# Four diagonal taps instead of six for the last two convolution tiles, output weight casts behind the operands' high halves, and four more low halves made in layer 0

## The chip, the cores and the metric

The kernel runs on one core of a Trainium2 chip. The metric is device time in microseconds for one execution on that core; three runs of the kernel before are shown, and one more execution was profiled.

## The reference, cut to what matters

One sequence of 512 tokens and width 1024 goes through two layers, all in float32. Layer 0 has a state-space branch and an attention branch behind one input projection (`e_w_in`) and one output projection (`e_w_out`, from 2048 to 1024 columns). Layer 1, in which most of the change lies, is this:

```python
def conformer_conv_layer(x, g_pre, w_in, conv_w, conv_b, ln_g, ln_b, w_out, g_post):
    u = rmsnorm(x, g_pre)
    proj = jnp.einsum('bsd,de->bse', u, w_in)                 # 1024 -> 3 x 2048
    val, glu_gate, z = jnp.split(proj, [D_CONV, 2 * D_CONV], axis=-1)
    h = val * jax.nn.sigmoid(glu_gate)
    h = causal_depthwise_conv(h, conv_w, conv_b)              # 31 taps in each of 2048 channels
    h = jax.nn.silu(layernorm(h, ln_g, ln_b))                 # over the 2048 channels of a token
    h = h * jax.nn.silu(z)
    out = jnp.einsum('bse,ed->bsd', h, w_out)                 # 2048 -> 1024
    return x + rmsnorm(out, g_post)
```

## The kernel before, in words

**Split products.** A float32 product is made of three matmuls in a faster 32-bit format (`mm3`): each operand is split into a high half, which is a cast on ACT, and a low half, which is the operand less that cast, a subtraction on DVE or POOL. The matmuls are high times high, high times low, low times high. For weights the cast is `w<-wr` (or `ws<-wr` in smaller tiles), from the raw tile `wr` that a DMA brings, and the subtraction is `w<-wr,w` (line 189). For the operands of the output projections the halves are `hlh` and `hll` (function `hilo`, line 119).

**Jobs.** The weights come in tiles of 128 x 1024 (512 KB). Each is a `Job`, and `run` takes the jobs in order, feeding PE in chunks; `split_to` makes the halves of the next jobs and `load_to` issues their loads on SP's queue. Three raw tiles are held at a time, so a raw load waits until the job three places earlier has been cast and subtracted. There are seven large weight tiles; two of them hold gates of layer 1 for a while. A weight tile can also have its low half made ahead: `lo_ahead`, a generator of which `run` takes a step every so many chunks in layer 0, loads a raw tile (`pre`, three buffers), casts it (`prh`), subtracts in place (`pre<-pre,prh`) and stores the result in DRAM (`lo`). In layer 1 such a job loads its low half from there (`w<-lo`) and needs only the cast. This is done for the 48 jobs of `o_w_in`. What is left over of the generator runs at the end of layer 0. A `pre` load waits until the store three places earlier has left its buffer.

**Order.** PE keeps the order in which the program is written. The other engines' rows are placed by a scheduler that goes by priority and dependence; `tc.issue_after(x)` keeps an instruction behind `x`. `cast` puts a weight cast behind the PSUM evacuation (`evacuated`) of three jobs before.

**Layer 1's convolution.** Channels lie in 16 tiles of 128. The 31 taps of a tile are divided: DVE runs `acc<-h,cw,acc` (line 982) on a PSUM accumulator, two tiles interleaved; POOL adds products that ACT makes (`acc<-acc,prod`, line 889), `NPT` counts these; and for the last two tiles, 14 and 15, PE runs `NPE` = 6 taps as matmuls with a diagonal matrix `dg` that ACT makes (`tap_job`; `acc<-h,dg` in float32). Such a tile's PE result is copied by ACT and added by POOL (line 897). The parts are joined in `cvo` (line 987), squared on ACT (line 996), and summed into `Ssum` and `Qsum` (line 1005).

**Statistics and output projection.** PE's `st` matmuls add up the sums over the channels. DVE and POOL make mean and reciprocal deviation from them, PE spreads these over the partitions (`mu`, `rs`), and between these steps PE runs the last three of the `z` jobs. Then each tile goes through `lnorm` (two DVE instructions, lines 1080 and 1081, and a silu on ACT, `s<-cvo`), `lgate` (POOL, `s<-s,sz`, line 1086) and `hilo`. The 16 output jobs, called job 0 to job 15 here, take two of these operands each in the first eight. The first four use small weight tiles (`ws`).

**Layer boundary.** At the end of layer 0 the output projection's last five jobs run together, 128 tokens (a block) after the other. Each block is then normed: its square sum on ACT, `y` (line 708), the variance `var` (line 344), a power on POOL, the residual (line 712, spilled to DRAM), another norm that gives `u` (line 365). PE transposes `u` (`uT`), ACT and DVE take the halves `uh` and `ul` (lines 390, 397), and layer 1 starts. Blocks 0 and 1 are transposed before the last matmuls of block 3.

Of the kernel before, what the change touches and what calls it, by code (L numbers as in the profile page):

```python
# [36 lines left out]
def trunk(  # L37
# [7 lines left out]
    V, G, A, T = nc.vector, nc.gpsimd, nc.scalar, nc.tensor  # L45
    x, out = x[0], out[0]
    e_w_in, e_w_out, o_w_in, o_w_out = e_w_in[0], e_w_out[0], o_w_in[0], o_w_out[0]
# [14 lines left out]
    LA = 6  # L62
    LB = 5
    LC = 3
# [4 lines left out]
    def nm(s):  # L69
        uid[0] += 1  # L70
        return f"{s}_{uid[0]}"

    def t2(s, dt=F32):
        return tp.tile([P, S], dt, tag="t", name=nm(s))
# [4 lines left out]
    def bank(s):  # L79
        return pp.tile([P, S], F32, tag="b", name=nm(s))  # L80
# [4 lines left out]
    def f32(t):  # L85
        return t.bitcast(F32)
# [27 lines left out]
    def tok(b):  # L114
        return slice(b * P, (b + 1) * P)

    def split(hi, lo, src, hi_eng, lo_eng):
        hi_eng(hi, src)
        lo_eng.tensor_tensor(lo, src, f32(hi), ALU.subtract)  # L119

    def hilo(src, n=S, eng=None, s="hl", cast=None):
        h, l = t2(s + "h", F32R)[:, :n], t2(s + "l", F32R)[:, :n]
        split(h, l, src, cast or A.copy, eng or V)
        return h, l
# [13 lines left out]
    def unspill(d, s):  # L138
        t = t2(s)
        nc.sync.dma_start(t, d)  # L140
        return t
# [1 line left out]

    last_load, last_cast = [None], [None]

    evacs = []

    def evacuated(i):
        evacs.append((state["run"], i.ins))

    def cast(hi, src):
        done = [i for n, i in evacs if n <= state["split"] - 3]
        if done:
            with tc.issue_after(done[-1]):
                last_cast[0] = A.copy(hi, src).ins  # L155
        else:
            last_cast[0] = A.copy(hi, src).ins  # L157
# [19 lines left out]
    def wsplit(j):  # L177
        _, _, nk, _, n = j.spec
        hl = j.hl if j.lo is not None else wtiles(j.small)
        w = 1024 // len(hl[0])  # L180
        for i in range(len(hl[0])):
            src = j.raw[:, i * w : (i + 1) * w]
            if j.lo is not None:
                cast(hl[0][i], src)
            else:
                cast(hl[0][i], src)
                for c in range(0, w, S if j.eng is G else w):
                    sl = slice(c, c + (S if j.eng is G else w))
                    j.eng.tensor_tensor(hl[1][i][:, sl], src[:, sl], f32(hl[0][i])[:, sl], ALU.subtract)  # L189
        m = w // n  # L190
        return [lambda k, t=t: t[k // m][:, k % m * n : (k % m + 1) * n] for t in hl]

    def lo_ahead(js):


        def load(j):
            w, r0, nk, c0, n = j.spec
            t = ep.tile([P, 1024], F32, tag="e", name=nm("pre"))
            with tc.issue_after(last_load[0]):
                nc.sync.dma_start(t.rearrange("p (k f) -> p k f", k=nk),  # L200
                                  w[r0 : r0 + nk * P, c0 : c0 + n].rearrange("(k p) f -> p k f", p=P))
            return t

        def sub(t):
            h = eh.tile([P, 1024], F32R, tag="eh", name=nm("prh"))
            for i in range(2):
                sl = slice(i * S, i * S + S)
                with tc.issue_after(last_cast[0]):
                    A.copy(h[:, sl], t[:, sl])  # L209
                V.tensor_tensor(t.bitcast(F32R)[:, sl], t[:, sl], f32(h)[:, sl], ALU.subtract)  # L210

        def store(j, t):
            j.lo = lop.tile([P, 1024], F32, tag="lo", name=nm("lo"))
            nc.sync.dma_start(j.lo, t)
        loaded = []
        for i in range(len(js) + 2):
            if i > 1:
                sub(loaded[i - 2])
            if i > 2:
                store(js[i - 3], loaded[i - 3])  # L220
            if i < len(js):
                loaded.append(load(js[i]))
            yield
        store(js[-1], loaded[-1])

    jobs = []
    state = dict(loaded=0, split=0, run=0)
    ahead = {}

    class Job:  # L230
        def __init__(self, w, r0, nk, c0, n, run, eng=None):
            self.spec, self.run, self.make = (w, r0, nk, c0, n), run, None if w is not None else eng
            self.lo = None
            jobs.append(self)
            self.eng = eng or (V if len(jobs) % 2 else G)
            self.small = False
            if w is not None and eng is V and len(jobs) % 16 in GLO:
                self.eng = G
# [21 lines left out]
    def chunks():  # L260

        i = state["run"]
        split_to(i + 1)
        first = True
        for _ in jobs[i].run(*jobs[i].w):
            if first:
                split_to(i + 1 + ahead.get(i, 2))
                first = False
            yield
        state["run"] = i + 1  # L270

    early = iter(())
    done = {}
# [54 lines left out]
    def run(n, after=None):  # L328

        for _ in range(n):  # L330
            for c, _ in enumerate(chunks()):
                if after is not None:
                    after()
                i = state["run"]
                if 5 <= i < 13 or 26 <= i:
                    if (8 * i + c) % (16 if i >= JO else 7 if i >= 26 else 8) == 0:
                        next(early, None)


# [420 lines left out]
    JO = len(jobs)  # L760
    out_proj(e_w_out, [(lambda k: hilo(yT.pop(k) if k < KT else oT.pop(k - KT), eng=G if k < KT else V), 2)],
             16, gpost, resid0, done0, {(3, 7): start1, (2, "end"): 1, (3, "end"): 1})
    J1 = len(jobs)
# [4 lines left out]
    acc, hs, part, pv, sz = {}, {}, {}, {}, {}  # L768
    sums = []
    NPS = [0] * 8  # L770
    NPT = [10]*7+[8]
    NPE = [0]*7+[6]
    PACE_DVE = 1.03
    PACE_POOL = 0.45
    LEAD = 8
# [67 lines left out]
    def tap_job(j):  # L843

        n = NPE[j // 2]

# [19 lines left out]
    def pool_adds(js, s0, n, init):  # L866

        a2 = {}
        prs = {}

        def prod(i):
            if i < n * len(js):
                j, s = js[i % len(js)], s0 + i // len(js)
                prs[i] = t2("prod")
                A.activation(prs[i][:, s:], hs[j][:, : S - s], AF.Copy, scale=w31(30 - s, j))  # L875
        for j in js:
            a2[j] = t2("acc2")
            if init:
                A.activation(a2[j], hs[j], AF.Identity, bias=c1[:, o_cb1 + j : o_cb1 + j + 1], scale=w31(30, j))
            else:  # L880
                s = s0 + n
                A.activation(a2[j][:, :s], ones[:, :s], AF.Identity, scale=0.0)
                A.activation(a2[j][:, s:], hs[j][:, : S - s], AF.Copy, scale=w31(30 - s, j))
        for i in range(3):
            prod(i)
        for i in range(n * len(js)):
            prod(i + 3)
            j, s = js[i % len(js)], s0 + i // len(js)
            G.tensor_tensor(a2[j][:, s:], a2[j][:, s:], prs.pop(i)[:, s:], ALU.add)  # L889
            yield  # L890
        for j in js:
            if NPE[j // 2]:
                while ("t", j) not in pacc or clock[0] < pacc["t", j] + 1:
                    yield
                pr = t2("prod")
                A.copy(pr[:, 1:], pacc[j][:, 1:])
                G.tensor_tensor(a2[j][:, 1:], a2[j][:, 1:], pr[:, 1:], ALU.add)
                yield
            part.setdefault(j, []).append((a2[j], clock[0]))

    def pool_halves(js):

        n = NPT[0] - 1
        s1 = n + 1
# [28 lines left out]
    def pool_stream():  # L933
        yield from pool_halves((0, 1))
        for j in range(2, NT):
            while j not in hs or clock[0] < hs["t", j] + (3 if j > 1 else 0):
                yield
            yield from pool_adds((j,), 1 + NPE[j // 2], NPT[j // 2] - 1, False)

# [5 lines left out]
    def lane(l):  # L945
        for j in range(l, NT, 2):
            if j < 2:
                m = NPT[0]
                a, b = bank("acc"), c1[:, o_cb1 + j : o_cb1 + j + 1]
# [19 lines left out]
            h = hs[j]  # L969
            n, m, e = NPS[j // 2], NPT[j // 2], NPE[j // 2]  # L970
            s = n + m + e + 1
# [19 lines left out]
    def tile_end(j, a):  # L991
        o = acc[j]
        if not NPT[j // 2]:
            A.copy(o, a)
# [39 lines left out]
    for j in range(NT):  # L1034
        val_job(j)
        gate_job(j)
        while zi < min(NT, j - LEAD + 2):
            z_job(zi)
            zi += 1
    rest = [j for j in range(NT) if NPE[j // 2]]  # L1040
    while zi < NT or rest:
# [5 lines left out]
    JO1 = len(jobs)  # L1047
# [28 lines left out]
    act1 = {}  # L1076
# [8 lines left out]
    def lgate(j):  # L1085
        G.tensor_tensor(act1[j], act1[j], sz[j], ALU.mult)

    def done1(b, y1):
        for f in range(2):
            nc.sync.dma_start(out[tok(b), f * S : (f + 1) * S], y1[f])  # L1090

    out_proj(o_w_out, [(lnorm, LA), (lgate, LB), (lambda j: hilo(act1.pop(j)), LC)],
             NT, gpost1, lambda b: [unspill(d, "x1") for d in x1[b]], done1, {})


# [410 lines left out]

    for j in jobs[6:40]:
        j.eng = G
    early = lo_ahead([j for j in jobs[J1:] if not j.make][:48])
    run(1)  # L1510
    steps = Steps()
    steps.until = JO + 3
# [82 lines left out]
```

## Time and profile before

| | us |
|---|---|
| three runs | 942.18, 944.03, 947.37 (median 944.03) |
| the profiled execution | 945.71 |
| its span | 943.9 |
| PE busy | 909.5 (96%) |
| PE weight loads busy | 754.9 (80%) |
| DVE busy | 730.7 (77%) |
| ACT busy | 601.2 (64%) |
| POOL busy | 506.5 (54%) |
| DMA | 159.84 MB, mean 169 GB/s |

The profiled execution's own time is 1.8 us above its span, since the span runs from the first to the last instruction. A row of the timeline gives start, duration, engine, line, instruction, tile written and tiles read, the shape, and how many alike were put together; in square brackets stands how long the engine was idle ahead of it and what ended that. Matmuls overlap each other, so the durations of single matmuls add up to more than the time that passes, and their start times are what to read. Layer 0 runs to about 563 us, the convolution to about 816, the output projection from 843 on.

### The profile page before, as it was taken

Reading aid. Unit: us, or ns where it says so; the run is one execution under the profiler, and the core shown is the slowest. Engines: PE = TensorE matmul, PEld = TensorE weight load, DVE = VectorE, ACT = ScalarE, POOL = GpSimd, SP = SyncE. Lnnn points to the kernel's source line nnn. Section 1 sums busy time; section 2 is a strip of 40 time slices with the busy share of each in tenths; the row PEclk is TensorE's granted clock in tenths of the full one; section 3 lists DMA queues with packets and bytes.
Section 4 is the critical chain, followed back from the end, with each engine's and each line's share of the span. In section 5 each row is a group of like instructions: output and inputs, shape, how many; then the busy total and the mean of one; then the engine's idle time right before and its main releaser. Section 6 shows DMA issues by size and latency. Waiting matters only on the chain.

```text
span 943.9 us, 13899 instructions
## 1 busy us (share of the span) xinstructions
PE 909.5 (96%) x4691; PEld 754.9 (80%) x4691; DVE 730.7 (77%) x1278; ACT 601.2 (64%) x1128; POOL 506.5 (54%) x474
## 2 busy tenths in 40 slices
PE   6999999998999999999899999999999999998997
PEld 5987787787898888788678889888888887785785
DVE  5657968778977887988776257999999999589602
ACT  5757667567846766576675437787876869456400
POOL 2604554535642444345573114898999999346410
PEclk9999999999999999999999999999999999999999
DMA  6726632347764574664347993565565664425303
GB/s 208 230 73 186 194 90 66 91 144 236 222 214 146 179 241 141 201 225 163 130 144 248 322 320 104 169 191 160 184 211 160 212 194 127 157 76 170 134 1 111
DMA packets 180267, 159.84 MB, mean 169 GB/s; under 512 B 7708, under 2 KB 151716, under 8 KB 180196
## 3 DMA queue, kind: packets, MB, share of 16 engines
q1 hardware_dynamic: 180180, 158.96, 53.0%
q8 instruction: 37, 0.61, 0.3%
q14 instruction: 34, 0.28, 0.1%
q10 hardware_dynamic: 16, 0.00, 0.0%
HBM read 129.45 MB, written 29.36 MB: 168 GB/s over the span
## 4 chain that ended last, share of the span: by engine, by line
PE 45%; DVE 7%; issue 3%; ACT 1%; DMA 1%; POOL 1%; DVEq 0%; POOLq 0%; ACTq 0%
PE m L102 28%; PE o L102 14%; DVE hll L119 1%; PE acc L102 1%; DVE w L189 1%; DVE pre L210 1%; PE tm L102 1%; DVE cvo L1081 1%; PE s L102 1%; DVE cvo L1080 1%; DMA pre<-in_o_w_in_dram 0%; PE pT L106 0%; ACT pr L95 0%; DMA wr<-in_e_w_out_dram 0%; DMA lo<-pre 0%
## 5 line engine op out<-in xcount | busy, mean ns | idle before, releaser
L102 PE MATMUL m<-uh,w 128*128 128x512 f32 (+1 forms) x1392 | 452.6, 392 | 0.4 <-DVE w L189 0.4
L102 PEld LDWEIGHTS m<-uh,w 128*128 128x128 f32 x1392 | 260.8, 189 | 51.4 <-issue 3.1
L102 PE MATMUL m<-ul,w 128*128 128x512 f32 (+1 forms) x696 | 267.3, 384 | 0.0
L189 POOL TENSOR_TENSOR w<-wr,w 128x512 fp32r<-128x512 f32 x112 | 158.7, 1441 | 159.0 <-ACT w L157 123.3
L982 DVE SCALAR_TENSOR_TENSOR acc<-h,cw,acc 128x490 f32<-128x490 f32 (+14 forms) x272 | 177.9, 738 | 3.4 <-ACT acc L974 2.6
L889 POOL TENSOR_TENSOR acc<-acc,prod 128x505 f32<-128x505 f32 (+12 forms) x122 | 156.3, 1283 | 8.1 <-ACT prod L875 0.8
L102 PEld LDWEIGHTS m<-ul,w 128*128 128x128 f32 x696 | 131.9, 189 | 21.3 <-issue 0.5
L102 PE MATMUL o<-w,hlh 128*128 128x512 f32 x448 | 141.4, 397 | 2.7 <-ACT pr L95 2.3
L210 DVE TENSOR_TENSOR pre<-pre,prh 128x512 fp32r<-128x512 f32 x96 | 83.0, 879 | 34.7 <-ACT prh L209 34.4
L102 PEld LDWEIGHTS o<-w,hlh 128*128 128x128 f32 x448 | 82.8, 189 | 19.2 <-ACT pr L95 3.1
L102 PE MATMUL tm<-w,uh 128*128 128x256 f32 (+1 forms) x384 | 91.7, 330 | 1.9 <-ACT pr L95 0.9
L157 ACT CAST w<-wr 128x1024 fp32r<-128x1024 f32 x72 | 74.8, 1048 | 28.6 <-PE o L102 7.9
L1457 POOL TENSOR_SCALAR pr<-pr,ri 128x128 f32<-128x128 f32 (+1 forms) x64 | 40.0, 626 | 92.8 <-DVE ri L1456 87.2
L102 PE MATMUL o<-w,hll 128*128 128x512 f32 x224 | 88.0, 393 | 0.8 <-DVE hll L119 0.8
L209 ACT CAST prh<-pre 128x512 fp32r<-128x512 f32 x96 | 56.8, 622 | 34.6 <-DVE pre L210 12.4
L875 ACT ACTIVATE prod<-h,cw 128x505 f32<-128x505 f32 (+12 forms) x122 | 77.7, 708 | 0.0
L346 POOL TENSOR_TENSOR rstd<-var,mhalf 128x1 f32<-128x1 f32 (+1 forms) x20 | 13.6, 680 | 112.4 <-DVE var L344 112.4
L155 ACT CAST w<-wr 128x1024 fp32r<-128x1024 f32 x56 | 57.4, 1051 | 18.9 <-PE o L102 11.8
L102 PEld LDWEIGHTS tm<-w,uh 128*128 128x128 f32 x384 | 62.8, 190 | 7.6 <-ACT pr L95 1.1
L102 PE MATMUL tm<-w,ul 128*128 128x256 f32 (+1 forms) x192 | 61.2, 319 | 0.0
L95 ACT ACTIVATE pr<-s,nmx 128x128 f32<-128x128 f32 (+1 forms) x64 | 33.9, 530 | 37.4 <-DVE nmx L1451 28.2
L102 PEld LDWEIGHTS o<-w,hll 128*128 128x128 f32 x224 | 42.3, 189 | 11.0 <-DVE hll L119 2.0
(270 smaller groups left out, 1607.1 us busy)
## 6 DMA issues: line engine op xcount, KB each, us to landing
wr<-in_e_w_in_dram SPq DMA_DIRECT2D x56, 512.0 KB
pre<-in_o_w_in_dram SPq DMA_DIRECT2D x48, 512.0 KB
lo<-pre SPq DMA_DIRECT2D x48, 512.0 KB
wr<-in_o_w_in_dram SPq DMA_DIRECT2D x48, 512.0 KB
w<-lo SPq DMA_DIRECT2D x44, 512.0 KB
wr<-in_e_w_out_dram SPq DMA_DIRECT2D x16, 512.0 KB
wr<-in_o_w_out_dram SPq DMA_DIRECT2D x16, 512.0 KB
x<-in_x_dram SPq DMA_DIRECT2D x12, 256.0 KB
```

What stands on the lines that cost most here:

```text
L95: i = A.activation(*a, **kw)
L102: T.matmul(o, l, r, start=start, stop=stop, skip_group_check=True)
L155: last_cast[0] = A.copy(hi, src).ins
L157: last_cast[0] = A.copy(hi, src).ins
L189: j.eng.tensor_tensor(hl[1][i][:, sl], src[:, sl], f32(hl[0][i])[:, sl], ALU.subtract)
L209: A.copy(h[:, sl], t[:, sl])
L210: V.tensor_tensor(t.bitcast(F32R)[:, sl], t[:, sl], f32(h)[:, sl], ALU.subtract)
L346: mark["rstd"] = G.tensor_tensor(r, v, mhalf.to_broadcast([P, ss.shape[-1]]), ALU.pow).ins
L875: A.activation(prs[i][:, s:], hs[j][:, : S - s], AF.Copy, scale=w31(30 - s, j))
L889: G.tensor_tensor(a2[j][:, s:], a2[j][:, s:], prs.pop(i)[:, s:], ALU.add)
L982: V.scalar_tensor_tensor(a[:, s:], h[:, : S - s], w31(30 - s, j), a[:, s:], ALU.mult, ALU.add)
L1457: G.tensor_scalar(p[:, :L], p[:, :L], ri, 1.0, ALU.mult, ALU.mult)
```

## The change

Three edits, and a fourth that paces the third. `NPE` goes from 6 to 4 for the last two tiles and `NPT` from 8 to 9. So DVE's first tap of these tiles is one earlier, and POOL has one more product. The casts of the output weights are placed behind the high half that was issued last (`act_last`), in place of an evacuation three jobs before. And `lo_ahead` is given four more tiles, the output jobs 4 to 7, with a step every 11 chunks in place of 16 in the output projection of layer 0.

```diff
-    evacs = []
+    evacs, act_last = [], [None]
...
     def cast(hi, src):
         done = [i for n, i in evacs if n <= state["split"] - 3]
+        if state["split"] >= JO1 and act_last[0] is not None:
+            done = act_last
         if done:
             with tc.issue_after(done[-1]):
                 last_cast[0] = A.copy(hi, src).ins
...
-                    if (8 * i + c) % (16 if i >= JO else 7 if i >= 26 else 8) == 0:
+                    if (8 * i + c) % (11 if i >= JO else 7 if i >= 26 else 8) == 0:
                         next(early, None)
...
-    NPT = [10]*7+[8]
-    NPE = [0]*7+[6]
+    NPT = [10] * 7 + [9]
+    NPE = [0] * 7 + [4]
...
+    def lparts(j):
+        def high(h, src):
+            act_last[0] = A.copy(h, src).ins
+        return hilo(act1.pop(j), cast=high)
+
...
-    out_proj(o_w_out, [(lnorm, LA), (lgate, LB), (lambda j: hilo(act1.pop(j)), LC)],
+    out_proj(o_w_out, [(lnorm, LA), (lgate, LB), (lparts, LC)],
              NT, gpost1, lambda b: [unspill(d, "x1") for d in x1[b]], done1, {})
...
-    early = lo_ahead([j for j in jobs[J1:] if not j.make][:48])
+    early = lo_ahead([j for j in jobs[J1:JO1] + jobs[JO1 + 4 : JO1 + 8] if not j.make])
```

Lines of the changed kernel are two to seven higher than those named above. Three places show how rows move.

DVE in the output projection, from low half 3 on. Before (`w_9203`, `w_9334`, `w_9381` and `w_9424` are the weights of jobs 4 to 7):

```order
L189 TENSOR_TENSOR w_9203<-wr_9130,w_9203 128x1024
L119 TENSOR_TENSOR hll_9216<-s_9083,hlh_9215 128x512
L1081 TENSOR_TENSOR cvo_8469<-cvo_8469,rs_9062 128x512
L189 TENSOR_TENSOR w_9334<-wr_9167,w_9334 128x1024
L119 TENSOR_TENSOR hll_9237<-s_9092,hlh_9236 128x512
L189 TENSOR_TENSOR w_9381<-wr_9206,w_9381 128x1024
L119 TENSOR_TENSOR hll_9258<-s_9101,hlh_9257 128x512
L1080 TENSOR_TENSOR cvo_8640<-cvo_8640,mu_9057 128x512
L189 TENSOR_TENSOR w_9424<-wr_9337,w_9424 128x1024
L119 TENSOR_TENSOR hll_9279<-s_9201,hlh_9278 128x512
```

The same place in the changed kernel, again from low half 3 on:

```order
L119 TENSOR_TENSOR hll_9254<-s_9117,hlh_9253 128x512
L1083 TENSOR_TENSOR cvo_8505<-cvo_8505,rs_9096 128x512
L1083 TENSOR_TENSOR cvo_8676<-cvo_8676,rs_9096 128x512
L119 TENSOR_TENSOR hll_9275<-s_9126,hlh_9274 128x512
L1082 TENSOR_TENSOR cvo_8773<-cvo_8773,mu_9091 128x512
L1082 TENSOR_TENSOR cvo_8916<-cvo_8916,mu_9091 128x512
L119 TENSOR_TENSOR hll_9296<-s_9135,hlh_9295 128x512
L1083 TENSOR_TENSOR cvo_8773<-cvo_8773,rs_9096 128x512
L1083 TENSOR_TENSOR cvo_8916<-cvo_8916,rs_9096 128x512
L119 TENSOR_TENSOR hll_9317<-s_9239,hlh_9316 128x512
```

The four weight subtractions are gone from between the low halves, and the norm's instructions stand in pairs.

ACT at the last sums of the convolution, from the last products of tile 15 on. Before (the copy on line 896 is of tile 15's PE taps, the two squares are of tiles 14 and 15):

```order
L875 ACTIVATE prod_8863<-h_1748_8746,cw 128x499
L996 ACTIVATE sq_8882<-cvo_8861 128x512
L896 COPY prod_8908<-acc_8847 128x511
L95 ACTIVATE sz_8917<-m_8873 128x512
L155 CAST w_8852<-wr_8850 128x1024
L996 ACTIVATE sq_8950<-cvo_8900 128x512
```

And in the changed kernel, where that copy is on line 898:

```order
L877 ACTIVATE prod_8906<-h_1760_8782,cw 128x500
L998 ACTIVATE sq_8936<-cvo_8916 128x512
L95 ACTIVATE sz_8946<-m_8896 128x512
L157 CAST w_8881<-wr_8879 128x1024
L898 COPY prod_8962<-acc_8876 128x511
L95 ACTIVATE sz_8983<-m_8948 128x512
L157 CAST w_8903<-wr_8901 128x1024
L998 ACTIVATE sq_9002<-cvo_8961 128x512
```

The copy now stands behind a silu and a weight cast, and so does the last square behind one more of each.

DVE at the layer boundary, block 1, from the square sums' addition to the first `ul`. Before:

```order
L709 TENSOR_TENSOR ss_6163<-ss_6163,ss_5863 128x1
L344 TENSOR_SCALAR var_6169<-ss_6163 128x1
L712 SCALAR_TENSOR_TENSOR o_1242_5862<-o_1242_5862,rstd_6171,x_6052 128x512
L712 SCALAR_TENSOR_TENSOR y_1319_6166<-y_1319_6166,rstd_6171,x_6053 128x512
L362 TENSOR_TENSOR s_1326_6181<-s_1326_6181 128x1
L344 TENSOR_SCALAR var_6187<-s_1326_6181 128x1
L365 TENSOR_SCALAR u_6179<-o_1242_5862,rstd_6189 128x512
L365 TENSOR_SCALAR u_6180<-y_1319_6166,rstd_6189 128x512
L397 SCALAR_TENSOR_TENSOR ul_1336_6256<-uT_6271,c_135,uh_1335_6255 128x256
```

And in the changed kernel:

```order
L711 TENSOR_TENSOR ss_6192<-ss_6192,ss_5881 128x1
L212 TENSOR_TENSOR pre_6102<-pre_6102,prh_6247 128x512
L346 TENSOR_SCALAR var_6198<-ss_6192 128x1
L212 TENSOR_TENSOR pre_6102<-pre_6102,prh_6247 128x512
L714 SCALAR_TENSOR_TENSOR o_1248_5880<-o_1248_5880,rstd_6200,x_6070 128x512
L714 SCALAR_TENSOR_TENSOR y_1329_6195<-y_1329_6195,rstd_6200,x_6071 128x512
L364 TENSOR_TENSOR s_1336_6210<-s_1336_6210 128x1
L346 TENSOR_SCALAR var_6216<-s_1336_6210 128x1
L367 TENSOR_SCALAR u_6208<-o_1248_5880,rstd_6218 128x512
L367 TENSOR_SCALAR u_6209<-y_1329_6195,rstd_6218 128x512
L212 TENSOR_TENSOR pre_6178<-pre_6178,prh_6339 128x512 x2
L399 SCALAR_TENSOR_TENSOR ul_1346_6285<-uT_6300,c_135,uh_1345_6284 128x256
```

Low halves of two more tiles stand in the block's chain, one around the variance, one between `u` and `ul`; ACT has their casts (`prh`) at the same places, the second ahead of `uh`.

## The prediction

> **What bounds the kernel now.** I read the busy time by stretches first, since a share over the whole span mixes stages. The columns are the stretch, its length, then busy PE, PEld, DVE, ACT and POOL with their counts, the granted clock, the DMA share and GB/s.
>
> ```profile
> 540.00:550.00 10.00, 10.00 (x45) 8.26 (x44) 5.32 (x13) 3.91 (x10) 1.44 (x2) 1.00 0.94 322
> 550.00:560.00 10.00, 10.00 (x47) 8.27 (x46) 2.84 (x9) 1.39 (x4) 1.10 (x2) 1.00 0.97 342
> ...
> 700.00:750.00 50.00, 50.00 (x222) 41.40 (x221) 48.76 (x78) 37.89 (x61) 48.12 (x39) 1.00 0.58 182
> ...
> 840.00:860.00 20.00, 17.24 (x76) 13.54 (x74) 20.00 (x25) 14.40 (x22) 9.33 (x6) 1.00 0.41 135
> 860.00:880.00 20.00, 17.67 (x74) 13.22 (x73) 20.00 (x19) 12.62 (x19) 15.62 (x9) 1.00 0.38 129
> ```
>
> PE is full at the layer boundary (540 to 560) and in the convolution (700 to 750), so matmuls taken out there shorten the run as long as nothing else is late. From 840 to 880, where the last projection starts, DVE is full and PE is not: there the low halves decide. The chain that ended last says the same (start, length, what):
>
> ```profile
> 790.97 5.12 PE acc L102 x12
> ...
> 801.54 5.12 PE acc L102 x12
> ...
> 823.00 1.68 PE st L102 x16
> ...
> 877.27 53.70 PE o L102 x236
> ```
>
> It runs through both tap blocks without a wait, and from 877 to 931 it is PE alone. Between these lie PE's waits (engine, releaser: us in all, times, longest; window 838 to 900), of which the first is shown with the rows around it:
>
> ```profile
> PE o L102 <- DVE hll L119: 5.1, 5, 1.8
> ```
> ```profile
> 842.82 0.61 PE L102 MATMUL o<-ws,hlh 128*128 128x512 f32 x2
> 843.27 0.39 PE L102 MATMUL o<-ws,hll 128*128 128x512 f32 x1
> ...
> 850.98 0.63 PE L102 MATMUL o<-ws,hlh 128*128 128x512 f32 x2
> 853.43 0.50 PE L102 MATMUL o<-ws,hll 128*128 128x512 f32 x1 [1.82 <-DVE hll L119]
> ```
>
> An undisturbed low-half matmul starts 0.45 us after its pair (842.82, 843.27); this one starts 2.45 after, 2.00 late, where the idle entry says 1.82. With that 0.17 on each of five waits, PE loses 5.1 + 0.85 = 5.95 us.
>
> **Taps, part by part.** Each block has 12 records for six taps in 5.12 us, 0.853 us a tap. Two taps fewer in each of two blocks: 4 x 0.853 = 3.41 us off PE in a stage where PE ends last. Cover for what comes instead: per tile one tap more on DVE, one product more on ACT and one add more on POOL (and two diagonals fewer on ACT). They end in the sums that PE's "st" matmuls read.
>
> ```profile
> 792.55 3.79 DVE L982 SCALAR_TENSOR_TENSOR acc<-h,cw,acc 128x490 f32<-128x490 f32 x5
> 797.16 14.24 DVE L982 SCALAR_TENSOR_TENSOR acc<-h,cw,acc 128x497 f32<-128x497 f32 x20 [0.81 <-ACT acc L974]
> ...
> 815.99 0.69 DVE L1005 TENSOR_TENSOR Qsum<-Qsum,sq 128x512 f32<-128x512 f32 x1
> 824.71 0.17 DVE L1058 TENSOR_SCALAR mq<-st 128x8 f32<-128x8 f32 x1 [8.03 <-PE st L102]
> ```
> ```profile
> 800.88 9.28 POOL L889 TENSOR_TENSOR acc<-acc,prod 128x505 f32<-128x505 f32 x7
> 813.27 1.29 POOL L897 TENSOR_TENSOR acc<-acc,prod 128x511 f32<-128x511 f32 x1 [3.11 <-ACT prod L896]
> ```
>
> The sums are done at 816.7 and PE reaches "st" at 823.0: 6.3 us in hand. PE will come 3.41 earlier, at 819.6. On POOL an add costs 9.28 / 7 = 1.33; two of them move its end from 810.2 to 812.8, and DVE's sums of tile 14, which now fall among its adds, push it to about 814; the add of the PE taps (1.29) ends near 815.3, no longer waiting 3.11 us, since its copy on ACT comes at about 812.9 (after the square of tile 14, one silu and one weight cast). DVE's taps take 0.71 to 0.76 us each, two more are 1.5; then the last join, two sums: about 817.3. Slack left: about 2 us. I take the whole 3.41; the other end is 3.41 less what the sums are late, down to 0.
>
> **Operands.** Six vector subtractions for output weights stand among the low halves now, and leave that place: those of jobs 4 to 7 come from DRAM, job 8's stands ahead of the last low half only, job 10's behind it. What they cost:
>
> ```profile
> 850.91 1.87 DVE L189 TENSOR_TENSOR w<-wr,w 128x1024 fp32r<-128x1024 f32 x1
> 852.70 0.68 DVE L119 TENSOR_TENSOR hll<-s,hlh 128x512 fp32r<-128x512 f32 x1
> ...
> 858.37 1.79 DVE L119 TENSOR_TENSOR hll<-s,hlh 128x512 fp32r<-128x512 f32 x1
> ```
> ```profile
> 858.24 1.36 POOL L1086 TENSOR_TENSOR s<-s,sz 128x512 f32<-128x512 f32 x1 [1.48 <-ACT s L95]
> ```
> ```profile
> 844.02 0.59 ACT L95 ACTIVATE sz<-m 128x512 f32<-128x512 f32 x1
> 848.56 1.05 ACT L155 CAST w<-wr 128x1024 fp32r<-128x1024 f32 x1 [3.95 <-DMA wr<-in_o_w_out_dram]
> 849.51 0.81 ACT L95 ACTIVATE s<-cvo,c 128x512 f32<-128x512 f32 x1
> 850.23 0.60 ACT L118 CAST hlh<-s 128x512 fp32r<-128x512 f32 x1
> ```
> ```profile
> 844.32 0.68 DVE L189 TENSOR_TENSOR ws<-wr,ws 128x512 fp32r<-128x512 f32 x1
> ```
> ```profile
> 845.02 40.28 SPq L161 DMA_DIRECT2D wr<-in_o_w_out_dram  x12
> ```
>
> The subtraction at 850.91 is what low half 3 (852.70) waited for. It does not become free of waits: ACT's cast for job 4 still stands ahead of high half 3 and still waits for its raw weights, whose transfer starts when job 1's last subtraction on DVE frees a buffer (844.32 + 0.68, issue at 845.02), unchanged. In the frame 3.41 us earlier the cast starts at 845.15; one silu that moves behind it (0.5 of its 0.59), then activation and high half (0.72 + 0.6) end it near 847.9. DVE is there at 848.1. PE wants low half 3 at 850.98 + 0.45 - 3.41 = 848.02. Alone it takes 0.68, PE is 0.75 late; but a low half that meets a gate product takes 1.79 and ends 0.56 after POOL does (859.60, 860.16): then it ends at 849.2 and PE is 1.3 us late. I take 1.3, since gate 6 follows the activation by nothing. From there one operand costs POOL 1.36 and DVE 0.56 in turn, 1.9 us, and PE takes one per 12 matmuls, 12 x 53.70 / 236 = 2.73, so no later one is late. Saved: 5.95 - 1.3 = 4.65. The ends are 2 (job 4's raw weights come a little later) and 5.95.
>
> The Trainium skill, SBUF — State Buffer, section "Who interferes with whom", says that a DVE instruction with two SBUF inputs and a GpSimd one that reads SBUF exclude each other for a whole instruction. By that rule the saving is the 4.65, without it 5.2; the 1.79 against 0.68 above agrees.
>
> The casts themselves: four are later on ACT (job 5's after high half 8, near 854); PE wants job 5 at about 868. The two preloads queued on SP ahead of job 4's raw weights wait for PE jobs that end by 834, before the buffer they would hold up is free (841.6): nothing. The lo loads (4 x 0.5 MB) land among the last z jobs, in a stretch whose neighbour has a DMA share of 0.41: nothing.
>
> **Four more low halves in layer 0.** Eight casts (0.58 each) and eight subtractions (0.69) more, on engines that are busy 14 to 53% of a stage where PE is full; the price is in the transfers. Each adds 1.05 MB (a load and a store of 512 KB) to a stage at 322 to 342 GB/s. The last two loads now come after the spill at 546, since each waits for an earlier store to leave its buffer, and two DVE subtractions of the first of them stand ahead of the variance of block 1, two of the other ahead of ul.
>
> ```profile
> 532.19 1.24 SPq L214 DMA_DIRECT2D lo<-pre  x1
> ...
> 538.63 0.38 SPq L200 DMA_DIRECT2D pre<-in_o_w_in_dram  x1
> ...
> 546.07 0.32 SPq L135 DMA_DIRECT2D x<-o  x1
> ```
> ```profile
> 542.83 1.15 ACT L209 CAST prh<-pre 128x512 fp32r<-128x512 f32 x2 [0.55 <-DMA pre<-in_o_w_in_dram]
> ```
> ```profile
> 543.48 0.69 DVE L210 TENSOR_TENSOR pre<-pre,prh 128x512 fp32r<-128x512 f32 x1 [0.42 <-ACT prh L209]
> ...
> 550.11 0.15 DVE L344 TENSOR_SCALAR var<-ss 128x1 f32<-128x1 f32 x1
> ...
> 554.67 0.48 DVE L365 TENSOR_SCALAR u<-y,rstd 128x512 f32<-128x512 f32 x1
> ```
> ```profile
> 559.75 1.91 PE L106 MATMUL uT<-ident,u 128*128 128x128 f32 x16
> ```
>
> A store took up to 6.4 us (532.19 to 538.63), a load 4.2 (to 542.83). So: load at about 547, landed at 551, cast and subtraction 1.3, variance at 552.3 in place of 550.1, u done at 557.4, PE's transposes at 559.75. 2.3 us remain; the second load lands near 554, its subtractions end before ul is wanted. Cost 0; the bound is a stall of what the load is later than 553.4.
>
> **Sum.** 3.41 + 4.65 = 8.1. The profiled execution took 945.71 (span 943.9 and 1.8 around it): 937.6. It is 1.7 above the median of the three runs, 944.03, which becomes 935.9, so 936.
>
> **Rivals.** (1) The boundary decides. If all added bytes (4 x 1.05 = 4.2 MB) pushed these loads back at the stage's rate, 4.2 / 0.33 = 12.7 us, PE would stall 12.7 - 2.3 = 10.4: 944.0 - 8.1 + 10.4 = 946.3, slower; it passes zero where the load lands after 561.5. Against it: half of the added work goes ahead of 530, since a step is taken every 11 chunks and not 16. 5% for this (3 of them beyond half a per cent), 10% for a stall of 1 to 4 us (937 to 940).
>
> The Trainium skill, DMA: Bandwidth & Descriptors, "Where 436 GB/s comes from", puts HBM at about 358 GB/s a core, which would leave the boundary almost nothing; by it the added bytes are an estimated 11.7 us and the time 945.3.
>
> (2) The operands stay late: job 4's raw weights or ACT pace the low halves, PE waits as long as now. For it: ACT sat 3.95 us for that transfer. Only the taps remain: 940.6; 12%. (3) The sums are late: about 2 us of slack left after five hand-overs between DVE, ACT and POOL; if the square waits behind a silu for PE, up to 3.4 are lost: 939.4; 8%. Against it: each is worked out from rows with the engines idle after it. My forecast: 65%, by itself 933.5 to 938.5.
>
> **Numbers.** Half a per cent, about what a measurement of this kernel can tell from no change, is 4.7 us: 939.3. Faster: 65, half of the small stalls (5) and half of case 3 (4), 74%; slower 3%; the same 23%. Range 933 (all waits gone, 9.4 saved, and a run's scatter) to 941 (taps alone).
>
> **What would show it.** Right: tap blocks of 8 records in 3.4 us; DVE's wait for "st" near 4 us, not 8; one PE wait for a low half near 1.1 us, at number 3; uT without a wait. Wrong: "st" waiting for Qsum; uT or ul waiting behind "pre" on ACT or DVE; several waits for hll left.

## Result and the profile after

The changed kernel takes 939.89 us in the median of eight executions (937.29 to 942.07), the kernel before 946.13 in the median of eight beside them (942.18 to 948.67; the three of the forecast are among them). The ratio is 0.9942, 95% interval 0.9927 to 0.9956: faster by 6.2 us by the medians and by 5.5 by the ratio, 4.2 to 6.9 by the interval, where the forecast said 8.1. The profiled execution took 940.86, its span is 939.1.

The same stretches as before (stretch, length, busy PE, PEld, DVE, ACT, POOL with counts, granted clock, DMA share, GB/s):

```profile
540.00:550.00 10.00, 10.00 (x46) 8.29 (x45) 3.76 (x9) 3.51 (x9) 0.88 (x1) 1.00 0.76 267
550.00:560.00 10.00, 9.86 (x45) 7.93 (x43) 4.13 (x10) 1.79 (x5) 1.42 (x2) 1.00 0.92 306
...
840.00:860.00 20.00, 19.01 (x83) 15.09 (x83) 20.00 (x32) 15.46 (x26) 12.27 (x9) 1.00 0.34 120
860.00:880.00 20.00, 20.00 (x90) 16.58 (x89) 16.32 (x13) 12.66 (x17) 15.12 (x10) 1.00 0.47 159
```

From 840 to 880 PE is now busy 39.0 of 40 us, where it was 34.9. The chain that ended last (start, length, what) shows both halves of the gain: tap blocks of 8 records, and a last stretch that PE alone sets 24 us earlier than before.

```profile
794.95 3.42 PE acc L102 x8
...
803.85 3.42 PE acc L102 x8
...
823.64 1.68 PE st L102 x16
...
853.51 72.74 PE o L102 x320
```

PE's waits in the output projection (us in all, times, longest; window 838 to 900), and then those about the layer boundary (530 to 600):

```profile
PE o L102 <- DVE hll L119: 0.7, 1, 0.7
PE o L102 <- ACT hlh L1092: 0.3, 1, 0.3
```
```profile
PE uT L106 <- DVE u L367: 2.8, 1, 2.8
```

Five waits for low halves became one, and a new one stands at uT. Executions differ by where the granted clock falls for a while (0.57 from 460 to 464 us in the kernel before, 1.00 there in taps_only), so a total says little about one edit. What says more is the time between fixed rows on PE: the first "uT" (the transposes of blocks 0 and 1), the first tap block, the first "st", the first o matmul with small weights, and the end of the last chain of o. Each number is the difference of two start times of the timeline.

| kernel | uT to taps | taps to st | st to o | o to its end |
|---|---|---|---|---|
| before | 231.06 | 32.03 | 19.98 | 88.15 |
| after | 235.30 | 28.70 | 19.98 | 82.79 |
| difference | +4.24 | -3.33 | 0.00 | -5.36 |

With uT itself 0.27 earlier, these make the 4.7 us by which the end of o moved (930.97 to 926.25). So the taps gave what they were priced at, the operands gave more, and the boundary took back half in this execution. Two kernels below (casts_and_lo, cast4_later) run the same layer 0, and in their traces the boundary took 1.5 and 1.6 us (232.59 and 232.68 in the first column), so 4.24 is the dearest of three.

### The profile page after: what moved, and what is told of

It reads as the page before. It is cut to its first block, busy times and chain, and to the rows that moved or that the text cites. A ratio compares the mean times of both kernels' runs of the same rounds, so it can differ in the third digit from the quotient of the medians.

```text
span 939.1 us, 13909 instructions
## 1 busy us (share of the span) xinstructions
PE 906.6 (97%) x4683; PEld 755.6 (80%) x4683; DVE 731.1 (78%) x1284; ACT 605.3 (64%) x1134; POOL 511.6 (54%) x476
## 4 chain that ended last, share of the span: by engine, by line
PE 42%; DVE 6%; DMA 5%; issue 2%; ACT 2%; SPq 1%; POOL 1%; DVEq 0%; POOLq 0%; ACTq 0%
PE m L102 29%; PE o L102 10%; DMA lo<-pre 3%; DVE pre L212 2%; DMA wr<-in_o_w_in_dram 1%; PE acc L102 1%; PE tm L102 1%; DMA wr<-in_e_w_out_dram 1%; DVE w L191 1%; PE s L102 1%; DVE pl L119 1%; PE pT L106 0%; DMA pre<-in_o_w_in_dram 0%; ACT pr L95 0%; DMA pre<-in_o_w_out_dram 0%
## 5 line engine op out<-in xcount | busy, mean ns | idle before, releaser
L984 DVE SCALAR_TENSOR_TENSOR acc<-h,cw,acc 128x490 f32<-128x490 f32 (+13 forms) x274 | 179.0, 731 | 2.7 <-ACT acc L976 2.0
L891 POOL TENSOR_TENSOR acc<-acc,prod 128x507 f32<-128x507 f32 (+9 forms) x124 | 159.6, 1289 | 8.2 <-ACT prod L877 0.7
L212 DVE TENSOR_TENSOR pre<-pre,prh 128x512 fp32r<-128x512 f32 x104 | 90.6, 889 | 44.8 <-ACT prh L211 44.6
L211 ACT CAST prh<-pre 128x512 fp32r<-128x512 f32 x104 | 61.2, 622 | 48.5 <-DMA pre<-in_o_w_in_dram 14.6
L877 ACT ACTIVATE prod<-h,cw 128x507 f32<-128x507 f32 (+9 forms) x124 | 79.0, 709 | 0.0
```

The source lines that it names most:

```text
L984: V.scalar_tensor_tensor(a[:, s:], h[:, : S - s], w31(30 - s, j), a[:, s:], ALU.mult, ALU.add)
```

## Experiments

Medians in us; "before" is the kernel before, run beside each (945.7 to 946.1).

| kernel | median | ratio to before, 95% interval |
|---|---|---|
| taps_only | 941.42 | 0.9959 (0.9944 to 0.9974) |
| casts_only | 940.35 | 0.9937 (0.9918 to 0.9956) |
| lo_only_early | 938.62 | 0.9923 (0.9905 to 0.9941) |
| casts_and_lo | 943.65 | 0.9976 (0.9964 to 0.9987) |
| taps_casts | 938.50 | 0.9929 (0.9906 to 0.9953) |
| pace16 | 943.31 | 0.9976 (0.9957 to 0.9995) |
| cast4_later | 941.35 | 0.9960 (0.9942 to 0.9979) |
| earlier_steps | 936.94 | 0.9904 (0.9891 to 0.9917) |
| earlier_2taps | 940.74 | 0.9958 (0.9944 to 0.9973) |
| earlier_3taps | 935.04 | 0.9880 (0.9859 to 0.9901) |
| earlier_small3 | 935.35 | 0.9898 (0.9879 to 0.9917) |
| casts_taps_small3 | 936.16 | 0.9899 (0.9876 to 0.9922) |

**The taps alone.** To the kernel before:

```diff
-    NPT = [10]*7+[8]
-    NPE = [0]*7+[6]
+    NPT = [10] * 7 + [9]
+    NPE = [0] * 7 + [4]
```

> The kernel before with the taps' edit alone (four diagonal taps on PE in place of six, nine products on POOL in place of eight, for tiles 14 and 15). Theory: the matmuls taken out are worth what they took, 3.4 us: 946.1 becomes 942.7, ratio 0.9964; tap blocks of 8 records in 3.4 us, st does not wait for Qsum, the five waits for low halves stay (5.1 us). Rival: the sums end later than PE, st waits and the time stays within 1 us of before.

941.42, 4.5 us less, with an interval (2.5 to 5.3) that holds the 3.4. Taps to st takes 28.69, as in the changed kernel. The theory stands; the waits for low halves stay (3.4 us in three, where 5.1 in five had been expected).

**Casts and low halves without the taps.** To the changed kernel:

```diff
-    NPT = [10] * 7 + [9]
-    NPE = [0] * 7 + [4]
+    NPT = [10]*7+[8]
+    NPE = [0]*7+[6]
```

> The changed kernel with six diagonal taps as before (casts behind the high halves, four more low halves, a step every 11 chunks). Theory: the output projection saves 5.4 us and the layer boundary costs 4.2 (PE waits 2.8 for uT and then runs some us at a lower clock): 946.1 - 1.2 = 944.9, ratio 0.9987. Rival: the wait at the boundary belongs to the one profiled execution and does not count in the median: 946.1 - 5.4 = 940.7, ratio 0.9943.

943.65, 2.3 less than before: between the two. The trace says why. PE waits at uT, but for 1.26 us and not 2.81, and the clock stays at 1.00 behind it, where it fell in the changed kernel. First the row of this kernel, then the changed kernel's and its clock behind the wait:

```profile
563.29 1.75 PE L106 MATMUL uT<-ident,u 128*128 128x128 f32 x14 [1.26 <-DVE u L367]
```
```profile
562.67 2.29 PE L106 MATMUL uT<-ident,u 128*128 128x128 f32 x14 [2.81 <-DVE u L367]
```
```profile
560.00:565.00 5.00, 2.33 (x15) 2.33 (x16) 3.45 (x10) 4.01 (x12) 0.55 (x1) 0.87 0.94 347
565.00:570.00 5.00, 5.00 (x27) 4.35 (x27) 4.24 (x12) 2.03 (x7) 0.55 (x1) 0.79 1.04 295
```

uT to taps is 232.59 here, 1.5 over before, and 4.2 over in the changed kernel. Block 1's u is done at about the same time in both (563.6 and 563.0), since the load ahead of it sets it (ACT starts that cast at 557.02 here and at 556.40 there); PE came at 561.65 here and at 559.48 there. The boundary's price depends on how early PE gets there.

**The last loads taken away from the boundary.** To the changed kernel:

```diff
-                    if (8 * i + c) % (11 if i >= JO else 7 if i >= 26 else 8) == 0:
+                    if (8 * i + c) % (11 if i >= JO else 7 if i >= 26 else 6) == 0:
```

> The changed kernel, with a step of the low halves every 6 chunks in place of 8 in jobs 5 to 12 of layer 0, so that about three tiles more are made there and the last ones leave the boundary. Theory: the order of the last loads is what PE waited for; uT without a wait, 4.2 us less than the changed kernel: 935.7, ratio to before 0.989. Rival: the added bytes cost what they cost wherever they are moved; a wait of like size comes at another place of layer 0 and the time stays at 939 to 940 (0.993).

936.94, and the row is that of the kernel before, 16 transposes without a wait; uT to taps is 231.06 again, to the hundredth.

```profile
559.59 1.91 PE L106 MATMUL uT<-ident,u 128*128 128x128 f32 x16
```

Theory right, gain 3.0 by the medians (4.2 against the one profiled execution). The same bytes in layer 0, three tiles earlier, cost nothing that the trace shows.

**The opposite: more of them late.** To the changed kernel:

```diff
-                    if (8 * i + c) % (11 if i >= JO else 7 if i >= 26 else 8) == 0:
+                    if (8 * i + c) % (16 if i >= JO else 7 if i >= 26 else 8) == 0:
```

> The changed kernel with a step every 16 chunks in place of 11 in the output projection of layer 0, so that more of the four tiles is left for its end. Theory: what PE waits for at uT is the chain of loads and stores of these tiles; with two or three of them instead of one and a half behind the spill the wait grows by 4 us a tile, to 6 to 12 us: 943 to 949. Rival: the wait of the changed kernel was a chance of one execution; the time stays at 940.

943.31, 3.4 more than the changed kernel; uT to taps 236.58, 5.5 over before. The theory had the sign, and the time at the lower end of its range, but not the place: the first transposes come without a wait, and it is ACT, in order, that stands before a load with two halves of uT still to cast behind it (the second row). PE then waits for that uh, and again at the transposes of blocks 2 and 3, 3.2 us in both (the last two lines, window 530 to 600) and not the 6 to 12 us of the theory; behind the wait for uh (it ends at 567.4) the clock was 0.71 and 0.86 from 568 to 576.

```profile
566.39 0.62 ACT L211 CAST prh<-pre 128x512 fp32r<-128x512 f32 x1 [3.62 <-DMA pre<-in_o_w_out_dram]
566.91 0.83 ACT L392 ACTIVATE uh<-uT,c 128x256 fp32r<-128x256 f32 x2
```
```profile
PE uT L106 <- DVE u L367: 1.7, 1, 1.7
PE m L102 <- ACT uh L392: 1.5, 1, 1.5
```

**Which edit freed the operands.** Three kernels. First the changed kernel without its third edit:

```diff
-                    if (8 * i + c) % (11 if i >= JO else 7 if i >= 26 else 8) == 0:
+                    if (8 * i + c) % (16 if i >= JO else 7 if i >= 26 else 8) == 0:
...
-    early = lo_ahead([j for j in jobs[J1:JO1] + jobs[JO1 + 4 : JO1 + 8] if not j.make])
+    early = lo_ahead([j for j in jobs[J1:] if not j.make][:48])
```

> The changed kernel without its third edit: 48 low halves in layer 0 and a step every 16 chunks, as before; taps and casts as changed. Theory: the casts alone free the operands, since the weights' subtractions follow the casts and only job 4's is left ahead of low half 3 (1.2 to 1.9 us more there); the boundary has no wait: 945.9 - 3.4 - 5.4 + 1.7 = 938.8, no slower than the changed kernel (939.9). Rival: the saving is the low halves' own, and the subtractions hold PE up as before: 945.9 - 3.4 = 942.5, with four or five waits for low halves.

938.50, no slower than with it (939.89). o to its end takes 82.70, against 82.79 with the four low halves. Then each edit alone, to the kernel before. The casts (with `lparts` as in the change):

```diff
+        if state["split"] >= JO1 and act_last[0] is not None:
+            done = act_last
```

> The kernel before with the second edit alone (output weight casts behind the operands' high halves). Theory: it carries all of the operands' saving: from the first o matmul to the end of the last one 82.7 us as in the changed kernel, where the kernel before has 88.1; 945.7 - 5.4 = 940.3. Rival: it needs the low halves too; 85 us or more there, 943 or above.

And the low halves, with the steps of earlier_steps:

```diff
-                    if (8 * i + c) % (16 if i >= JO else 7 if i >= 26 else 8) == 0:
+                    if (8 * i + c) % (11 if i >= JO else 7 if i >= 26 else 6) == 0:
...
-    early = lo_ahead([j for j in jobs[J1:] if not j.make][:48])
+    early = lo_ahead([j for j in jobs[J1:JO1] + jobs[JO1 + 4 : JO1 + 8] if not j.make])
```

> The kernel before with the third edit alone, and its steps earlier (every 6 chunks in jobs 5 to 12 of layer 0, every 11 in the output projection), so that the layer boundary has no wait. Theory: in the old order of the casts every high half up to the ninth still waits for one cast and its raw weights on ACT; taking the subtractions off DVE saves 2 us at most: 943.7 to 945.7. Rival: the subtractions were the cost, and the saving is 4 to 5 us: 941.

The casts alone gave 940.35, as expected. The low halves alone gave 938.62, and there my theory fell: they do the same work. Below, the first o matmul and the chain of o, of casts_only and then of lo_only_early; from 842.73 to 925.47 is 82.74, from 841.60 to 924.37 is 82.77, against 88.15 before.

```profile
842.73 0.62 PE L102 MATMUL o<-ws,hlh 128*128 128x512 f32 x2
```
```profile
852.74 72.73 PE o L102 x320
```
```profile
841.60 0.62 PE L102 MATMUL o<-ws,hlh 128*128 128x512 f32 x2
```
```profile
851.62 72.75 PE o L102 x320
```

Why either is enough: PE takes an operand in 2.73 us. In lo_only_early ACT still has a cast ahead of each high half:

```profile
849.80 1.05 ACT L155 CAST w<-wr 128x1024 fp32r<-128x1024 f32 x1 [0.15 <-DMA wr<-in_o_w_out_dram]
850.75 0.81 ACT L95 ACTIVATE s<-cvo,c 128x512 f32<-128x512 f32 x1
851.47 0.61 ACT L118 CAST hlh<-s 128x512 fp32r<-128x512 f32 x1
...
854.68 1.04 ACT L155 CAST w<-wr 128x1024 fp32r<-128x1024 f32 x1
```

Cast, activation and high half are 1.05 + 0.81 + 0.61 = 2.5, within 2.73. In the kernel before, the cast's subtraction on DVE came on top (1.2 to 2.1 for each, with low halves of 1.8 beside POOL). Take away either the subtractions or their place ahead of the operands, and DVE keeps up. The second of the two adds nothing: the two savings don't add up.

**The last wait, at operand 3.** To the changed kernel:

```diff
-    ahead[JO1 - 3], ahead[JO1 - 2], ahead[JO1 - 1], ahead[JO1] = 3, 4, 4, 4
+    ahead[JO1 - 3], ahead[JO1 - 2], ahead[JO1 - 1], ahead[JO1] = 3, 4, 4, 3
```

> The changed kernel, with the weights of output job 4 taken up three jobs ahead and not four, so that their cast on ACT stands behind high half 6 and no longer ahead of high half 3. Theory: that cast and its wait for the raw weights are the last reason for PE's waits at operand 3 (0.32 and 0.67 us): both vanish, 1.0 us less than the changed kernel (938.9, ratio to it 0.9989). Rival: low half 3 is held by the gate product on POOL, not by ACT: the wait of 0.67 stays and the time too.

941.35, not faster, and the wait grew: 2.64 us in one. High half 3 starts 2.4 us behind the first o matmul (844.35 - 841.95), where the changed kernel has 8.0 (851.45 - 843.46), and low half 3 comes later all the same (first ACT, then DVE, POOL and PE of this kernel).

```profile
844.35 0.61 ACT L1092 CAST hlh<-s 128x512 fp32r<-128x512 f32 x1
```
```profile
844.65 1.73 DVE L191 TENSOR_TENSOR ws<-wr,ws 128x512 fp32r<-128x512 f32 x1
...
852.63 0.68 DVE L119 TENSOR_TENSOR hll<-s,hlh 128x512 fp32r<-128x512 f32 x1
```
```profile
844.53 4.70 POOL L1088 TENSOR_TENSOR s<-s,sz 128x512 f32<-128x512 f32 x3 [2.15 <-ACT s L95]
```
```profile
853.37 0.50 PE L102 MATMUL o<-ws,hll 128*128 128x512 f32 x1 [2.64 <-DVE hll L119]
```

Both theories named the wrong engine. DVE's order puts six subtractions of small weights ahead of low half 3, four of them for jobs 2 and 3, which PE reaches after it. And since ACT no longer holds back the gate products, POOL runs beside them: in the changed kernel five of these six took 0.68 us, here one does and the others take 1.2 to 1.7. The Trainium skill, SBUF — State Buffer, section "Who interferes with whom", has a DVE instruction with two SBUF inputs and a GpSimd one that reads SBUF exclude each other; this is what that lock costs when it is moved onto the path. Then job 3's subtractions were moved behind low half 4, on earlier_steps:

```diff
-    ahead[JO1 - 3], ahead[JO1 - 2], ahead[JO1 - 1], ahead[JO1] = 3, 4, 4, 4
+    ahead[JO1 - 3], ahead[JO1 - 2], ahead[JO1 - 1], ahead[JO1] = 3, 3, 3, 2
```

> The kernel with earlier steps (936.9), and the last small weight tile (job 3) taken up later, so that its two subtractions on DVE stand behind low halves 3 and 4 and job 4's cast behind high half 6. Theory: DVE's own order, not ACT, held low half 3; it comes 1.3 us earlier, PE's waits at operand 3 (1.4 us together) go: 935.5. Rival: the wait moves on to a later operand or to job 3's weights, and the time stays at 936.9.

935.35. The rows at operand 3 carry no wait, but one of 0.63 comes at operand 5, and o to its end is 82.15 in place of 82.72. So 0.6 of the 1.4 us are shown, and the rival was right in part: some of the wait moved on. The medians' 1.6 is within their scatter. The same line in taps_casts, so without the third edit and its pace:

> The changed kernel without its third edit, and with job 3's small weights taken up later (as in the kernel with 935.4). Theory: the four low halves in layer 0 are not needed: 938.5 - 1.2 = 937.3 by the median of the kernel without them, 935.4 by the nearest kernel with them; 935.4 to 937.3. Rival: with job 3's subtractions moved in among the low halves, the subtractions of jobs 4 to 7 are too many for DVE, PE waits at later operands and it is 939 or more.

936.16, with nearly the interval of the kernel with the low halves; o to its end 82.19. The four subtractions left on DVE delay nothing.

**Fewer taps.** On earlier_steps, first two diagonal taps and ten products, then three and nine:

```diff
-    NPT = [10] * 7 + [9]
-    NPE = [0] * 7 + [4]
+    NPT = [10] * 7 + [10]
+    NPE = [0] * 7 + [2]
```

```diff
-    NPE = [0] * 7 + [4]
+    NPE = [0] * 7 + [3]
```

> The kernel with earlier steps (936.9), with two diagonal taps on PE and ten products on POOL for tiles 14 and 15. Theory: 3.4 us more off PE, but two more taps on DVE (1.5 us) end the sums later, and of the slack of 1.9 us nothing is left: st waits for Qsum for 3.0 us, 936.9 - 3.4 + 3.0 = 936.5. Rival: the sums keep ahead of PE and the taps pay in full again: 933.5.

> The kernel with earlier steps (936.9), with three diagonal taps on PE and nine products on POOL. Theory: PE comes 1.7 us earlier, the sums end 1.5 later (two DVE taps), so st waits 1.3 us, which is too short for the clock to fall (0.53 to 0.61 for 7 us behind the wait of 3.2): 936.9 - 1.7 + 1.3 = 936.5. Rival: a wait of any length costs its own length again in clock: 936.9 - 1.7 + 2.6 = 937.8.

With two, st waits, as forecast, 3.18 us, and the time is 3.8 over earlier_steps where 0.4 under it was forecast. Behind the wait the granted clock is about half for 8 us, and st to o takes 23.23, 3.2 more than in any other kernel:

```profile
819.27 1.02 PE L102 MATMUL st<-ones,Ssum 128*128 128x1 f32 x8 [3.18 <-DVE Ssum L1007]
```
```profile
820.00:824.00 4.00, 4.00 (x16) 3.58 (x16) 1.58 (x9) 1.52 (x3) 1.02 (x1) 0.53 0.60 210
824.00:828.00 4.00, 4.00 (x13) 3.10 (x12) 1.94 (x6) 0.00 (x0) 0.00 (x0) 0.61 0.19 49
828.00:832.00 4.00, 4.00 (x27) 3.64 (x26) 1.10 (x2) 0.60 (x1) 0.00 (x0) 1.00 0.46 147
```

The wait cost its own length a second time; 0.7 more stands in o to its end (83.40 against 82.72), where high half 3 comes late. With three taps there is no wait at all: taps to st is 26.92, 1.77 less, and the median 935.04. My 1.5 us for the two DVE taps was too much: against the first tap block, the sums end only 0.3 later than in the changed kernel (816.64 - 789.56 = 27.08, against 821.60 - 794.78 = 26.82). One reason is that tile 14's addition to Qsum no longer falls among POOL's adds: it took 0.68 (at 813.96), against 1.76 in the changed kernel (at 816.23). So this kernel doesn't tell the two views of the clock apart. Its median is the lowest here, within the scatter of earlier_small3's 935.35. Three taps and the later small weights together were not run.

## Why the prediction was right, and where not

**Taps: right.** 3.41 forecast, 3.33 measured (32.03 to 28.70). The slack too. Qsum ends at 821.60, DVE's wait for st is 3.75 where it was 8.03, PE reaches st at 823.48: 1.9 us left, 2.3 by the forecast's numbers (817.3 against 819.6).

```profile
820.91 0.69 DVE L1007 TENSOR_TENSOR Qsum<-Qsum,sq 128x512 f32<-128x512 f32 x1
825.35 0.17 DVE L1060 TENSOR_SCALAR mq<-st 128x8 f32<-128x8 f32 x1 [3.75 <-PE st L102]
```

**Operands: the saving right, its cause half right.** 5.36 for the forecast 4.65, within its ends. PE's only stall is at operand 3, where it was put:

```profile
852.10 0.73 PE L102 MATMUL o<-ws,hlh 128*128 128x512 f32 x2 [0.32 <-ACT hlh L1092]
853.51 0.50 PE L102 MATMUL o<-ws,hll 128*128 128x512 f32 x1 [0.67 <-DVE hll L119]
```

By issue times it is 1.4 us (due at 843.46 + 12 x 0.68 + 0.45 = 852.07, issued at 853.51), forecast 1.3. The 0.7 more lies in the kernel before. There the last of the five late low halves was due at 842.82 + 40 x 0.68 + 0.45 = 870.47 and was issued at 877.27, 6.80 late, where the forecast counted 5.95: beside the 0.17 ahead of each wait, the pair after it starts late too (0.34 us after the first such low half, 853.43 to 853.77, where 0.23 is usual). 6.80 - 1.44 is the 5.36. Two things were wrong. The step "those of jobs 4 to 7 come from DRAM" was given a part of the saving; beside the casts it adds nothing (82.74 in casts_only, 82.79 in the changed kernel). And job 4's cast on ACT was not the one reason for the stall. The forecast itself had DVE there at 848.1, after ACT at 847.9, and cast4_later shows that DVE alone would hold it.

**Layer boundary: the mechanism right, the term mis-sized.** The forecast said that PE stalls by what the load is later than 553.4, and put its landing at 551: cost 0. Rows of SP, ACT and DVE of the changed kernel:

```profile
541.24 0.38 SPq L202 DMA_DIRECT2D pre<-in_o_w_out_dram  x1
...
543.28 1.31 SPq L216 DMA_DIRECT2D lo<-pre  x2
...
551.97 0.38 SPq L202 DMA_DIRECT2D pre<-in_o_w_out_dram  x1
```
```profile
556.40 1.14 ACT L211 CAST prh<-pre 128x512 fp32r<-128x512 f32 x2 [6.12 <-DMA pre<-in_o_w_out_dram]
```
```profile
557.05 0.69 DVE L212 TENSOR_TENSOR pre<-pre,prh 128x512 fp32r<-128x512 f32 x1 [4.75 <-ACT prh L211]
557.66 0.15 DVE L346 TENSOR_SCALAR var<-ss 128x1 f32<-128x1 f32 x1
...
562.53 0.48 DVE L367 TENSOR_SCALAR u<-y,rstd 128x512 f32<-128x512 f32 x1
```

The load was issued at 551.97 and its cast began at 556.40: 3.0 late by the forecast's own bound, and PE waited 2.81. What failed is the issue time. The forecast's issue at about 547 is the store row of the kernel before (541.06, below) and 6.4 us for a store. In the changed kernel the store that frees the buffer was issued at 543.28, 2.2 later, and took 8.7 us until the load could go; the load itself took 4.4, near the forecast's 4.2.

```profile
541.06 1.34 SPq L214 DMA_DIRECT2D lo<-pre  x2
```

Three loads in a row waited so for their buffers, and SP stood 9.3 us for such stores, 2.8 in one wait before (first the changed kernel, then the kernel before; window 515 to 570):

```profile
SPq L202 <- DMA lo<-pre: 9.3, 3, 3.8
```
```profile
SPq L200 <- DMA lo<-pre: 2.8, 1, 2.8
```

The case that came true is the small stall of 1 to 4 us with its 937 to 940, given 10%. Its full form, with all added bytes on the path, did not: 946.3 against the measured 939.89, and earlier_steps moves the same bytes at 936.94. The Trainium skill, DMA: Bandwidth & Descriptors, section "Where 436 GB/s comes from", has about 358 GB/s of HBM a core, from which 945.3 had been worked out; the runs don't bear that time out. The trace of the kernel before has 400 GB/s in the stretch from 545 to 550.

**The level.** The three executions known to the forecast had a median of 944.03, the eight 946.13. The 936 was a right place for a kernel 8.1 under the first; under the second it would have been 938. That 939.89 lies within the range is in part luck: its upper end, 941, stood for another case (the taps alone), and the operands made up 0.7 of what the boundary took. Rivals 2 and 3 did not occur; the second would have left five waits, the third a wait at st.

## What to carry to other kernels

Two edits that take the same wait away are worth one of them: ask of each what would still wait if the other were there already, and run each alone. A buffer that goes in and out of DRAM turns over at the pace of its store plus its load, and where an engine works in order, the consumer of the late load holds up everything written behind it; move such work to a stretch where no one is due. Price an idle TensorE of about 3 us at up to twice its length: of three such waits here, the one of 3.18 us cost about 6.4, that of 2.81 cost 4.2, and that of 2.64 no more than itself.

## What the hardware showed that I had not expected

The clock falls behind short idle times of PE too, and not each time. 3.18 us idle: 0.53 and 0.61 in the next two stretches of 4 us, 3.2 us lost. 2.81: 0.87 and 0.79 in the stretches of 5 us that hold the wait and follow it; of the 4.24 us at the boundary 1.4 are more than the wait. 2.64, in cast4_later: 1.00 in the stretch that holds it and in the next (the first two lines below), and o to its end is 84.20, 1.4 over the changed kernel, which is what low half 3 is later there by start times (2.8 us against 1.4). 1.26: nothing. So a wait does not always cost its length again. And the same wait of 1.82 for low half 3 left the clock at 1.00 in the kernel before, though one of 0.94 follows it, and took it down in taps_only (the second fence is before, the third taps_only):

```profile
850.00:855.00 5.00, 2.36 (x11) 1.62 (x10) 5.00 (x8) 3.36 (x6) 2.44 (x3) 1.00 0.62 214
855.00:860.00 5.00, 5.00 (x24) 4.12 (x23) 5.00 (x9) 4.91 (x8) 4.07 (x3) 1.00 0.54 183
```
```profile
850.00:854.00 4.00, 2.18 (x11) 1.39 (x10) 4.00 (x6) 3.79 (x6) 2.59 (x2) 1.00 0.49 164
854.00:858.00 4.00, 3.06 (x14) 2.23 (x13) 4.00 (x3) 3.19 (x5) 2.13 (x2) 1.00 0.59 203
```
```profile
848.00:852.00 4.00, 3.29 (x9) 2.61 (x10) 4.00 (x5) 3.01 (x5) 3.30 (x2) 0.69 0.44 143
852.00:856.00 4.00, 4.00 (x17) 3.23 (x16) 4.00 (x5) 3.44 (x5) 1.34 (x2) 0.88 0.66 202
```

The Trainium skill, TensorE: Matmul & The Clock Gate, section "Why this matters for your kernels", asks for no idle gap of TensorE over about 3 us, else the clock goes back to half. The trace agrees at 3.18 (0.53 and 0.61). Below 3 us the clock fell behind 1.82 in one kernel and not behind 1.82 and 2.64 in two others; why stays open.
